# Layer 0's sink column written by ScalarE, the first transfers in another order, and the last product in two pieces

## The chip, the cores and the metric

The kernel runs on one core of a Trainium2 chip. The metric is the device time of one execution in microseconds; the median of three runs of the kernel before is 1686.93 us (1686.22 to 1688.71). The core has a matrix engine (TensorE, PE in the profile, with its weight loads as PEld), VectorE (DVE), ScalarE (ACT), GpSimd (POOL) and SyncE (SP), which here issues every transfer between the memories. Each engine works through its own list of instructions in order and waits where one of them needs what another engine or a transfer has not yet delivered.

## What is computed

Two layers over 512 latent tokens and 256 context tokens of width 1024, all in float32. Each layer modulates its input with vectors that come from a conditioning vector (`silu(c) @ w_ada + b_ada`), mixes tokens, normalises, and applies an MLP of width 4096 with a squared ReLU. Layer 0 mixes with windowed attention of 16 query heads over 2 key heads, whose softmax has one more logit per head, the sink, which gives weight to no value:

```python
hx = x * (1.0 + sc1) + sh1
hc = ctx * (1.0 + csc1) + csh1
...
def softmax_with_sink(s, sink):
    m = jnp.maximum(jnp.max(s, axis=-1, keepdims=True), sink)
    p = jnp.exp(s - m)
    return p / (jnp.sum(p, axis=-1, keepdims=True) + jnp.exp(sink - m))
...
x = layer_norm(alpha * x + g1 * ax, ln1_g[i], ln1_b[i])
fx = sqrelu_mlp(x * (1.0 + sc2) + sh2, mlp_w1[i], mlp_w2[i])
x = layer_norm(alpha * x + g2 * fx, ln2_g[i], ln2_b[i])
```

Layer 1 mixes with differential attention. The output is the 512 latent tokens after layer 1.

## The kernel before, in words

**Products.** Every large matrix product is made of three products of reduced precision (`mm3`, lines 321 to 324): a float32 operand is split into a high part (a cast by ScalarE) and a low part (raw minus high, a subtraction by VectorE), and high·high, low·high and high·low are added up in the same accumulator. `wsplit` (line 299) does this for a weight: a transfer into `w_raw`, the cast `w_h`, the subtraction `w_l` (line 312). The helpers `dv`, `ac`, `gp` (lines 259 to 269) issue one instruction on VectorE, ScalarE or GpSimd, so most instructions carry one of the lines 260, 264 and 268 in the profile; tile names tell them apart.

**What sets the order.** A planner (`Flow`, line 63) runs while the program is built. Jobs are generators with priorities; each says what it waits for, and the planner keeps a rough clock in which each instruction of the other engines has an assumed length (`dve`, `act`, `pool2`, `mm`, lines 209 to 222). The job that may go on by that clock writes its matrix products next. So the order on TensorE is fixed by the planner's assumptions. The orders on VectorE, ScalarE, GpSimd and SyncE are set afterwards by the scheduler of the tile framework. An instruction that is added or removed on ScalarE or VectorE in layer 0's attention therefore moves products on TensorE as well.

**The start (lines 736 to 846).** Work goes in four groups `g` of 256 input columns. `start_load(g)` issues four 512 KB pieces of `w_ada` (for the scale and the shift), two pieces of the transposed input `xT` (384 KB each), and, in the groups 0 and 2, half of the key and value weights (`a_wkv`), and always a quarter of the first half of `a_wq`. `ada_stream` (line 348) makes the modulation rows: TensorE products `ada_ps`, a copy `ada_rows` by ScalarE, a transposition `ada_t` by TensorE, which needs the unit matrix `identr` (cast by VectorE from `ident`), and three small VectorE instructions, which need `badaT`. Then `start_x` (line 785) makes `hx`: ScalarE writes the high part, VectorE computes the modulated value in place and then the low part (GpSimd for the context tokens). `kv_job` multiplies each 128-column slice `k` of `hx` with the key and value weights (eighteen products of 256 columns for each slice), `proj` does the queries. All transfers go through SyncE's one list; a transfer takes one of eight semaphores in turn and waits until the one that used it eight transfers earlier has landed.

**Layer 0's attention (`group`, line 974).** 24 groups (6 blocks of 128 queries by 4 quarters of the heads) of four heads. For each head: scores `s_ps` by TensorE; one VectorE instruction that adds the mask, stores the negated scores in `e` and gives their row minimum `nm`, started from the negated sink `nsink` (line 1009); a VectorE maximum that writes the sink's column `e[:, W_]` (line 1012); the exponential by ScalarE over all columns with `nm` as its bias, which also gives the sum (line 1015); a reciprocal on VectorE; the multiplication by it on GpSimd (line 1018). When all four heads are ready, TensorE transposes them (`pT_ps`), ScalarE and VectorE copy the transposed blocks in turn (`pT`), and TensorE multiplies with the values (`o_ps`). Between these, the planner puts query projections, modulation rows for later, and, in `out_proj` (line 1076), the first half of the output projection (`y_ps`, with `yg`, `y_s` and their statistics on VectorE).

**The end (`tok_product`, line 589, and `done4`, line 1554).** The last product of layer 1's MLP takes for each of four token blocks and each half of the 1024 columns 24 products of 512 columns into one accumulator. VectorE multiplies it with the gate (`g_tmp`), adds it to `acc`, and takes the statistics; for the second half of a block `done4` follows: aggregate, a power on GpSimd, two VectorE passes over `acc` and the transfer out.

Of the kernel before, what the change touches and what calls it, by code (L numbers as in the profile page):

```python
# [19 lines left out]
P = 128  # L20
# [214 lines left out]
def hybrid_block(ctx: ExitStack, tc: tile.TileContext, t: dict, out: bass.AP):  # L235
# [23 lines left out]
    def dv(n, deps, fn, lat=LAT, **kw):  # L259
        fn(**kw)  # L260
        return fl.op("D", dve(n), deps, lat)
# [327 lines left out]
    def tok_product(pool, src, W, seq, acc, gates, done=None, st=None, scale=1.0, extra=None, pre={}, sink=None,  # L589
                    late=(1,)):  # L590
# [4 lines left out]
        for i, (half, tb) in enumerate(seq):  # L595
            if half not in Ws:
                Ws[half] = W(half)
            if (half, tb) in pre:
                pt, give, u0 = pre[(half, tb)]
            else:  # L600
                yield sm_.ok
                pt, u0 = psm("y_ps"), 0
                give = lambda x, i=sm_.take(): sm_.give(i, x)
            left = {u for h, b in seq[i + 1:] if h == half for u in range(pre[(h, b)][2] if (h, b) in pre else 0, 4)}
# [45 lines left out]
    def mlp(l, hx, ready, apool, pool, ntok, acc, gates, done, extra, res, XR=0):  # L650
# [25 lines left out]
        for ch in range(4):  # L676
# [52 lines left out]
            if ch == 2:  # L729
# [3 lines left out]
                                   done if ch == 3 else None, extra=extra, sink=sum_up(ch, gates) if ch < 3 else None)  # L733
# [5 lines left out]
    badaT = load_const("badaT", [P, DEPTH, 6, KT], adap[0])  # L739
# [4 lines left out]
    with tc.tile_pool(name="qpool", bufs=6, side="right") as qpool, \  # L744
# [6 lines left out]
        nc.vector.tensor_copy(out=identr, in_=load_const("ident", [P, P], pool))  # L751
# [17 lines left out]
        def start_load(g):  # L769
            Wa = [ada_load(t["w_ada"][0, m, g, u], next(raws)) for m in (1, 0) for u in range(2)]  # L770
            xs = []
            for k in (2 * g, 2 * g + 1):
                x, gr, rr = next(raws)
                x = x[:, 0:TOK]
                xs.append((k, x, dma(TOK, [gr], out=x, in_=t["xT"][:, k]), rr))
            if g == 0:
                Wkv.append(wsplit(t["a_wkv"][0]))
            if g == 2:
                hl = [pool.tile([P, 1024], F32R, name="w_kv", tag="x4", bufs=3) for _ in range(2)]
                Wkv.append(wsplit(t["a_wkv"][1], hl=hl + [None, None]))  # L780
            Wq[0].append(wsplit(t["a_wq"][0, g]))
            return Wa, xs
# [70 lines left out]
        def setup():  # L853
# [3 lines left out]
            nc.sync.dma_start(out=mask, in_=t["mask"])  # L857

        lnT = load_const("lnT", [P, DEPTH, 4, KT])
# [114 lines left out]
        def group(n, tb, qd):  # L974
# [9 lines left out]
            for j in range(4):  # L984
# [21 lines left out]
                else:  # L1006
# [5 lines left out]
                d = dv(1, [d], nc.vector.tensor_tensor, out=e[:, W_:W_ + 1], in0=nsink[:, hd_:hd_ + 1], in1=nm,  # L1012
                       op=ALU.max)
                sm = small.tile([P, 1], F32, name="sm", tag="sm")
                a = ac(W_ + 200, [d], nc.scalar.activation, out=e[:, 0:W_ + 1], in_=e[:, 0:W_ + 1], func=AF.Exp,
# [638 lines left out]
```

## Time and profile before

The profiled execution of the kernel before took 1690.51 us, of which its span from the first to the last instruction is 1688.7 us. A profile row of the timeline gives the start in us, the length, the engine, the line, the operation, what it writes and reads, and, in brackets, how long the engine had been idle and what ended the wait.

| | |
|---|---|
| median of 3 runs | 1686.93 us |
| profiled execution, its span | 1690.51 us, 1688.7 us |
| mean granted TensorE clock in it | 0.991 |
| TensorE (PE) busy | 1617.0 us, 96% of the span |
| VectorE (DVE) busy | 956.7 us, 57% |
| ScalarE (ACT) busy | 658.2 us, 39% |
| GpSimd (POOL) busy | 344.4 us, 20% |

### The profile page before, as it was taken

How to read it: one execution, taken by the hardware profiler on the slowest of the kernel's cores; microseconds unless marked ns; L12 is line 12 of the kernel's file. 1: busy time of each engine (PE TensorE's matmuls, PEld its weight loads, DVE VectorE, ACT ScalarE, POOL GpSimd, SP SyncE). 2: the span in 40 equal slices, each digit the busy share in tenths (PEclk: the TensorE clock that was granted, in tenths of full speed). 3: DMA queues.
4: the chain of work that ended last, by engine and by line, in shares of the span. 5: the costliest groups of instructions: out<-in, count | busy, mean ns of one | idle time of the engine just before them, and what ended most of it. 6: DMA issues, size and time to landing. Idle time of an engine off the chain costs nothing.

```text
span 1688.7 us, 23443 instructions
## 1 busy us (share of the span) xinstructions
PE 1617.0 (96%) x9129; PEld 1392.0 (82%) x9129; DVE 956.7 (57%) x1811; ACT 658.2 (39%) x1281; POOL 344.4 (20%) x314
## 2 busy tenths in 40 slices
PE   6899999999999999999999999999989899999997
PEld 4787677789889889979978998999877788888886
DVE  3665787567756344344446777677656552332436
ACT  3454565362223113202316555555543533222230
POOL 1243544100001101243220223221101001103422
PEclk9999999999999999999999999999999899999999
DMA  9111451434445334234313122211133323132321
GB/s 365 42 51 37 170 175 35 136 125 130 145 138 162 100 125 150 100 113 139 109 59 110 51 69 67 69 45 38 47 113 111 102 80 120 63 125 75 112 88 50
DMA packets 57239, 174.77 MB, mean 103 GB/s; under 512 B 7144, under 2 KB 13096, under 8 KB 57128
## 3 DMA queue, kind: packets, MB, share of 16 engines
q1 hardware_dynamic: 57128, 173.27, 30.6%
q8 instruction: 72, 1.18, 0.3%
q14 instruction: 39, 0.32, 0.1%
HBM read 165.35 MB, written 7.90 MB: 103 GB/s over the span
## 4 chain that ended last, share of the span: by engine, by line
PE 74%; DVE 10%; issue 5%; ACT 4%; DMA 3%; POOL 3%; SPq 0%; POOLq 0%; DVEq 0%; ACTq 0%
PE y_ps L324 10%; PE y_ps L323 10%; PE y_ps L322 10%; PE h_ps L322 8%; PE h_ps L323 8%; PE h_ps L324 8%; PE o_ps L1031 2%; PE qkv_ps L322 2%; PE qkv_ps L323 2%; PE s_ps L1347 2%; PE qkv_ps L324 2%; DVE w_l L312 2%; PE pT_ps L1049 2%; DVE e L260 1%; PE o_ps L1385 1%
## 5 line engine op out<-in xcount | busy, mean ns | idle before, releaser
L264 ACT CAST w_h<-w_raw 128x1024 fp32r<-128x1024 f32 (+1 forms) x185 | 186.4, 1014 | 413.1 <-PE y_ps L324 208.6
L312 DVE TENSOR_TENSOR w_l<-w_raw,w_h 128x1024 fp32r<-128x1024 f32 (+1 forms) x185 | 220.9, 1205 | 220.6 <-ACT w_h L264 219.7
L323 PE MATMUL y_ps<-w_l,hid 128*128 128x512 f32 x640 | 252.9, 395 | 1.8 <-DVE w_l L312 1.7
L324 PE MATMUL y_ps<-w_h,hid 128*128 128x512 f32 x640 | 252.9, 395 | 0.7 <-DVE hid L260 0.7
L322 PE MATMUL y_ps<-w_h,hid 128*128 128x512 f32 x640 | 253.1, 395 | 0.0
L268 POOL TENSOR_TENSOR relu<-relu 128x768 f32<-128x768 f32 (+1 forms) x48 | 80.4, 1674 | 608.2 <-ACT relu L264 608.2
L324 PE MATMUL h_ps<-hx0m,w_l 128*128 128x384 f32 (+1 forms) x528 | 175.7, 333 | 1.6 <-DVE w_l L312 1.6
L322 PE MATMUL h_ps<-hx0m,w_h 128*128 128x384 f32 (+1 forms) x528 | 175.7, 333 | 0.2 <-ACT w_h L264 0.2
L323 PE MATMUL h_ps<-hx0m,w_h 128*128 128x384 f32 (+1 forms) x528 | 175.3, 332 | 0.0
L323 PEld LDWEIGHTS y_ps<-w_l,hid 128*128 128x128 f32 x640 | 120.4, 188 | 31.1 <-DVE w_l L312 3.3
L324 PEld LDWEIGHTS y_ps<-w_h,hid 128*128 128x128 f32 x640 | 120.4, 188 | 30.1 <-DVE hid L260 2.0
L322 PEld LDWEIGHTS y_ps<-w_h,hid 128*128 128x128 f32 x640 | 120.4, 188 | 28.7 <-ACT hid L264 0.4
L322 PE MATMUL qkv_ps<-w_h,hx 128*128 128x384 f32 (+1 forms) x384 | 127.8, 333 | 0.1
L323 PE MATMUL qkv_ps<-w_l,hx 128*128 128x384 f32 (+1 forms) x384 | 123.2, 321 | 0.3 <-DVE w_l L312 0.2
L324 PE MATMUL qkv_ps<-w_h,hx 128*128 128x384 f32 (+1 forms) x384 | 123.0, 320 | 0.0
L268 POOL TENSOR_TENSOR e<-e,sm 128x512 f32<-128x512 f32 (+2 forms) x96 | 94.1, 995 | 115.4 <-DVE sm L260 76.9
L322 PE MATMUL h_ps<-hx1m,w_h 128*128 128x512 f32 (+1 forms) x288 | 107.7, 374 | 3.6 <-ACT relu L264 3.6
L323 PE MATMUL h_ps<-hx1m,w_h 128*128 128x512 f32 (+1 forms) x288 | 107.3, 372 | 0.0
L324 PE MATMUL h_ps<-hx1m,w_l 128*128 128x512 f32 (+1 forms) x288 | 107.2, 372 | 0.0
L324 PEld LDWEIGHTS h_ps<-hx0m,w_l 128*128 128x128 f32 x528 | 99.1, 188 | 2.9 <-DVE w_l L312 2.9
L322 PEld LDWEIGHTS h_ps<-hx0m,w_h 128*128 128x128 f32 x528 | 99.1, 188 | 0.8 <-ACT w_h L264 0.6
L323 PEld LDWEIGHTS h_ps<-hx0m,w_h 128*128 128x128 f32 x528 | 99.1, 188 | 0.1
(225 smaller groups left out, 3112.6 us busy)
## 6 DMA issues: line engine op xcount, KB each, us to landing
w_raw<-in_w SPq DMA_DIRECT2D x128, 512.0 KB, 3.5
w_raw<-in_w_adaT SPq DMA_DIRECT2D x56, 512.0 KB, 3.5
w_raw<-in_w_ada SPq DMA_DIRECT2D x24, 512.0 KB, 4.0
w_raw<-in_b_w SPq DMA_DIRECT2D x32, 384.0 KB, 3.6
raw<-in_w_ada SPq DMA_DIRECT2D x16, 512.0 KB, 9.6
w_raw<-in_a_wq SPq DMA_DIRECT2D x8, 512.0 KB, 4.7
w_raw<-in_a_wo SPq DMA_DIRECT2D x8, 512.0 KB, 3.4
w_raw<-in_b_wo SPq DMA_DIRECT2D x8, 512.0 KB, 3.5
```

What stands on the lines that cost most here:

```text
L260: fn(**kw)
L264: fn(**kw)
L268: fn(**kw)
L312: last["split"] = nc.vector.tensor_tensor(**kw)
L322: nc.tensor.matmul(out=o, lhsT=lh, rhs=rh, start=start, stop=False)
L323: nc.tensor.matmul(out=o, lhsT=lh, rhs=rl, start=False, stop=False)
L324: last["pe"] = nc.tensor.matmul(out=o, lhsT=ll, rhs=rh, start=False, stop=stop)
L1031: nc.tensor.matmul(out=po[odd * HD:odd * HD + HD, 0:256], lhsT=vv[:, kb, kvh], rhs=pt_[:, odd * 256:odd * 256 + 256], start=(i == 0), stop ...
L1049: nc.tensor.transpose(out=pp[:, c * P:(c + 1) * P], in_=es[j][:, i * P:(i + 1) * P], identity=ident)
L1347: nc.tensor.matmul(out=sp[:, c * 512:c * 512 + 384], lhsT=qTt[:, tt, hl, qb * P:(qb + 1) * P], rhs=kS[:, tt, c * 384:c * 384 + 384], start ...
L1385: nc.tensor.matmul(out=po[:, qp * 256:(qp + 1) * 256], lhsT=vt[:, kb, vl], rhs=pt_[:, pl, a * 256:a * 256 + 256], start=(kp == 0 and pl == ...
```

## The change

Three edits, with what they move.

1. **The sink's column.** `nm` is a minimum that starts from `nsink`, so `nm` is never above `nsink`, and the maximum of the two is `nsink` itself. The VectorE maximum is replaced by a ScalarE copy of `nsink` into the column. The copy waits neither for the scores nor for `nm`; the exponential now waits for the scores' VectorE instruction and for the copy.
2. **The first transfers.** `ident` and `badaT` move behind the first four pieces of `w_ada`; the first half of `a_wkv` moves ahead of the first two pieces of `xT`; `lnT` moves behind `mask`, 34 transfers later.
3. **The last product.** The second half of the last token block is computed as two accumulators of 256 columns, each with its own gate and addition on VectorE; the statistics still take all 512 columns at once.

```diff
     def tok_product(pool, src, W, seq, acc, gates, done=None, st=None, scale=1.0, extra=None, pre={}, sink=None,
-                    late=(1,)):
+                    late=(1,), fine=False):
...
+            if fine and i == len(seq) - 1:
+
+                for c in range(2):
+                    if c:
+                        yield sm_.ok
+                        pt = psm("y_ps")
+                        give = lambda x, i=sm_.take(): sm_.give(i, x)
+                    cs_ = slice(half * 512 + c * 256, half * 512 + c * 256 + 256)
+                    tok = slice(tb * P, (tb + 1) * P)
+                    for u in range(4):
+                        w = Ws[half][u]
+                        yield w.t
+                        for k in (2 * u, 2 * u + 1):
+                            c_ = slice((k % 2) * 512 + c * 256, (k % 2) * 512 + c * 256 + 256)
+                            mm3(pt[:, 0:256], hxs(src, k, 0, tok), hxs(src, k, 1, tok), w.h[:, c_], w.l[:, c_], k == 0,
+                                k == KT - 1)
+                        p = fl.pe(6 * mm(256))
...
+                    tm = pool.tile([P, 256], F32, name="g_tmp", tag="tmp", bufs=2)
+                    m = dv(256, [p], nc.vector.tensor_tensor, out=tm, in0=pt[:, 0:256], in1=gates[0][:, cs_], op=ALU.mult)
+                    give(m)
+                    r = dv(256, [m], nc.vector.tensor_tensor, out=acc[tb][:, cs_], in0=acc[tb][:, cs_], in1=tm, op=ALU.add)
+                st[tb], r = stats(acc[tb], half, r, st.get(tb))
+                done(tb, st[tb], r)
+                continue
...
-    badaT = load_const("badaT", [P, DEPTH, 6, KT], adap[0])
+    badaT = adap[0].tile([P, DEPTH, 6, KT], F32, name="c_badaT")
...
-        nc.vector.tensor_copy(out=identr, in_=load_const("ident", [P, P], pool))
...
         def start_load(g):
             Wa = [ada_load(t["w_ada"][0, m, g, u], next(raws)) for m in (1, 0) for u in range(2)]
+            if g == 0:
+                nc.vector.tensor_copy(out=identr, in_=load_const("ident", [P, P], pool))
+                nc.sync.dma_start(out=badaT, in_=t["badaT"])
+                Wkv.append(wsplit(t["a_wkv"][0]))
             xs = []
             for k in (2 * g, 2 * g + 1):
                 x, gr, rr = next(raws)
                 x = x[:, 0:TOK]
                 xs.append((k, x, dma(TOK, [gr], out=x, in_=t["xT"][:, k]), rr))
-            if g == 0:
-                Wkv.append(wsplit(t["a_wkv"][0]))
...
             nc.sync.dma_start(out=mask, in_=t["mask"])
+            nc.sync.dma_start(out=lnT, in_=t["lnT"])
 
-        lnT = load_const("lnT", [P, DEPTH, 4, KT])
+        lnT = const.tile([P, DEPTH, 4, KT], F32, name="c_lnT")
...
-                d = dv(1, [d], nc.vector.tensor_tensor, out=e[:, W_:W_ + 1], in0=nsink[:, hd_:hd_ + 1], in1=nm,
-                       op=ALU.max)
+
+                d = [d, ac(1, [], nc.scalar.copy, out=e[:, W_:W_ + 1], in_=nsink[:, hd_:hd_ + 1])]
                 sm = small.tile([P, 1], F32, name="sm", tag="sm")
-                a = ac(W_ + 200, [d], nc.scalar.activation, out=e[:, 0:W_ + 1], in_=e[:, 0:W_ + 1], func=AF.Exp,
+                a = ac(W_ + 200, d, nc.scalar.activation, out=e[:, 0:W_ + 1], in_=e[:, 0:W_ + 1], func=AF.Exp,
                        scale=-1.0, bias=nm, accum_out=sm)
```

Where the instructions stand changes at three places that the prediction uses. The first is SyncE's list at the very start; `raw` are the buffers for `w_ada` and `xT`. Before:

```order
L283 DMA c_cT<-in_cT 128x16
L283 DMA c_badaT<-in_badaT 128x96
L283 DMA c_ident<-in_ident 128x128
L283 DMA c_lnT<-in_lnT 128x64
L275 DMA raw_119<-in_w_ada 128x1024
L275 DMA raw_121<-in_w_ada 128x1024
L275 DMA raw_123<-in_w_ada 128x1024
L275 DMA raw_125<-in_w_ada 128x1024
L275 DMA raw_127<-in_xT 128x768
L275 DMA raw_129<-in_xT 128x768
L275 DMA w_raw<-in_a_wkv 128x1024
```

And of the change, the same engine from the same place:

```order
L283 DMA c_cT<-in_cT 128x16
L275 DMA raw_114<-in_w_ada 128x1024
L275 DMA raw_116<-in_w_ada 128x1024
L275 DMA raw_118<-in_w_ada 128x1024
L275 DMA raw_120<-in_w_ada 128x1024
L283 DMA c_ident<-in_ident 128x128
L799 DMA c_badaT<-in_badaT 128x96
L275 DMA w_raw<-in_a_wkv 128x1024
L275 DMA raw_132<-in_xT 128x768
L275 DMA raw_134<-in_xT 128x768
```

Three small transfers stood ahead of the first `w_ada`; now none of them does, two follow the fourth `w_ada`, and `a_wkv` has passed both pieces of `xT`. The rest of SyncE's list up to the query weights keeps its order.

The second place is VectorE's list right after the first group's modulation, where it makes the low part of `hx` (`hx_91` before, `hx_90` in the change, from `raw_127` and `raw_129`, now `raw_132` and `raw_134`) and of the weights (`w_l`). Before:

```order
L260 TENSOR_SCALAR raw_127<-raw_127,mods_81 128x512
L260 TENSOR_SCALAR raw_127<-raw_127,mods_81 128x256
L260 TENSOR_TENSOR hx_91<-raw_127,hx_91 128x512
L260 TENSOR_SCALAR raw_129<-raw_129,mods_81 128x512
L260 TENSOR_SCALAR raw_129<-raw_129,mods_81 128x256
L260 TENSOR_TENSOR hx_91<-raw_129,hx_91 128x512
L312 TENSOR_TENSOR w_l<-w_raw,w_h 128x1024 x2
```

And of the change:

```order
L312 TENSOR_TENSOR w_l<-w_raw,w_h 128x1024
L260 TENSOR_SCALAR raw_132<-raw_132,mods_81 128x512
L260 TENSOR_SCALAR raw_132<-raw_132,mods_81 128x256
L260 TENSOR_TENSOR hx_90<-raw_132,hx_90 128x512
L260 TENSOR_SCALAR raw_134<-raw_134,mods_81 128x512
L260 TENSOR_SCALAR raw_134<-raw_134,mods_81 128x256
L260 TENSOR_TENSOR hx_90<-raw_134,hx_90 128x512
L312 TENSOR_TENSOR w_l<-w_raw,w_h 128x1024
```

The first `w_l` (of `a_wkv`) has gone from behind both slices of `hx` to ahead of them. On ScalarE its cast `w_h` has gone the same way, from behind the four instructions for `hx` to ahead of them.

The third place is TensorE's list at the end of layer 0's attention: the transpositions of the last group's heads, and what stands ahead of them. `e_3551`, `e_3585`, `e_3574` and `e_3625` are the last group's four heads before. Before:

```order
L1049 MATMUL pT_ps<-identr,e_3540 128x128
L998 MATMUL s_ps<-kT_117,qT_1791 128x256 x2
L1031 MATMUL o_ps<-pT,v_118 64x256 x4
L1049 MATMUL pT_ps<-identr,e_3551 128x128
L1049 MATMUL pT_ps<-identr,e_3585 128x128
L1049 MATMUL pT_ps<-identr,e_3574 128x128
L1049 MATMUL pT_ps<-identr,e_3625 128x128
```

And of the change, where the last group's heads are `e_3551`, `e_3593`, `e_3562` and `e_3604`; right ahead of the first row stand the scores of the last two heads (`s_ps`, four products) and then the six `y_ps` products of 512 columns of which this is the last:

```order
L324 MATMUL y_ps<-w_h,hx_93 128x512
L1078 MATMUL pT_ps<-identr,e_3473 128x128
L1078 MATMUL pT_ps<-identr,e_3516 128x128
L1078 MATMUL pT_ps<-identr,e_3484 128x128
L1078 MATMUL pT_ps<-identr,e_3527 128x128
L1060 MATMUL o_ps<-pT,v_113 64x256 x4
L1078 MATMUL pT_ps<-identr,e_3551 128x128
L1078 MATMUL pT_ps<-identr,e_3593 128x128
L1078 MATMUL pT_ps<-identr,e_3562 128x128
L1078 MATMUL pT_ps<-identr,e_3604 128x128
```

Between the last scores and the last group's transpositions stood four `o_ps` products; now six `y_ps` products, four transpositions of the group before and four `o_ps` products stand there. On VectorE, the scores of the last head stood behind `yg`, `y_s`, a `pT` copy and the statistics of an output block, with the low part of an `hx` between them and the maximum; in the change the scores of the last two heads follow each other directly. Between the start and this place many products of the two lists trade places; behind it the two lists of TensorE are the same up to the last product.

More of the change, by code (lines that the diff above doesn't have):

```diff
@@ L732, in mlp @@
                                    [(h_, tb) for h_ in range(2) for tb in range(ntb)], acc, gates,
[L733 removed]
+                                   done if ch == 3 else None, extra=extra, sink=sum_up(ch, gates) if ch < 3 else None,
+                                   fine=l == 1 and ch == 3)
     l0 = ExitStack()
```

2 lines of the change are left out of this document (added).

## The prediction

> **What bounds the kernel now.** First the page's engine totals.
>
> ```profile
> PE 1617.0 (96%) x9129; PEld 1392.0 (82%) x9129; DVE 956.7 (57%) x1811; ACT 658.2 (39%) x1281; POOL 344.4 (20%) x314
> ```
>
> TensorE is busy 96% of the span. No product is removed, so the change can win only the time in which TensorE waits (1688.7 − 1617.0 = 71.7 us), and only at the three places that it touches: the start, layer 0's attention, the tail. Next the timeline of the first 31 us:
>
> ```profile
> 1.19 0.42 SPq L283 DMA_DIRECT2D c_badaT<-in_badaT  x1
> ...
> 2.60 1.85 SPq L275 DMA_DIRECT2D raw<-in_w_ada  x4
> 3.58 0.23 DVE L751 CAST identr<-c_ident 128x128 fp32r<-128x128 f32 x1 [2.42 <-DMA c_ident<-in_ident]
> ...
> 8.17 1.08 PE L364 MATMUL ada_ps<-raw,cs 128*32 128x256 f32 x8 [0.56 <-DMA raw<-in_w_ada]
> 9.75 0.69 PE L388 MATMUL ada_t<-identr,ada_rows 128*128 128x128 f32 x2 [0.49 <-ACT ada_rows L264]
> 12.37 0.37 ACT L264 COPY ada_rows<-ada_ps 128x256 f32<-128x256 f32 x1 [2.67 <-PE ada_ps L364]
> ...
> 13.92 2.50 ACT L264 ACTIVATE hx<-raw,mods 128x512 fp32r<-128x512 f32 x4 [1.18 <-DVE mods L260]
> 14.77 0.91 DVE L260 TENSOR_SCALAR raw<-raw,mods 128x512 f32<-128x512 f32 x2 [0.88 <-ACT hx L264]
> 15.59 0.68 DVE L260 TENSOR_TENSOR hx<-raw,hx 128x512 fp32r<-128x512 f32 x1
> 16.33 1.98 ACT L264 CAST w_h<-w_raw 128x1024 fp32r<-128x1024 f32 x2
> 17.99 2.88 DVE L312 TENSOR_TENSOR w_l<-w_raw,w_h 128x1024 fp32r<-128x1024 f32 x2
> 19.79 0.58 PE L323 MATMUL kv_ps<-w_l,hx 128*128 128x256 f32 x1 [1.79 <-DVE w_l L312]
> 20.16 0.41 PE L324 MATMUL kv_ps<-w_h,hx 128*128 128x256 f32 x1
> 30.27 1.22 DVE L312 TENSOR_TENSOR w_l<-w_raw,w_h 128x1024 fp32r<-128x1024 f32 x1
> ```
>
> The first key and value products wait for the weight's low part, which VectorE makes only after both slices of `hx`. The third product, the first that needs a low `hx`, starts at 20.16; from there the timeline shows no such wait of TensorE until the stage ends near 58. Then its waits from 60 to 320 us, and ScalarE's longest from 60 to 313:
>
> ```profile
> PE pT_ps L1049 <- ACT pT L264: 2.9, 4, 0.9
> PE pT_ps L1049 <- POOL e L268: 2.2, 1, 2.2
> PE s_ps L994 <- DVE nm L260: 1.8, 3, 0.9
> ```
>
> ```profile
> ACT e L264 <- DVE e L260: 53.5, 45, 2.3
> ```
>
> The softmax is slow as a chain (ScalarE waits 53.5 us for VectorE, the maximum being the last link), but the planner puts other products under it, so only 6.9 us reach TensorE. The largest wait is the last group's:
>
> ```profile
> 309.40 0.47 DVE L260 CUSTOM_DVE_ANT_0 e<-s_ps,mask,nsink 128x256 f32<-128x256 f32 x1
> 309.52 0.55 PE L1049 MATMUL pT_ps<-identr,e 128*128 128x128 f32 x3
> ...
> 310.05 0.42 DVE L260 TENSOR_TENSOR hx<-o_ps,hx 128x256 fp32r<-128x256 f32 x1 [0.17 <-ACT hx L264]
> 310.39 0.15 DVE L260 TENSOR_TENSOR e<-nsink,nm 128x1 f32<-128x1 f32 x1
> 310.63 0.51 ACT L264 ACTIVATE e<-e,nm 128x257 f32<-128x257 f32 x1 [0.62 <-DVE e L260]
> ...
> 311.57 0.61 POOL L268 TENSOR_TENSOR e<-e,sm 128x256 f32<-128x256 f32 x1 [2.25 <-DVE sm L260]
> 312.24 0.77 PE L1049 MATMUL pT_ps<-identr,e 128*128 128x128 f32 x5 [2.17 <-POOL e L268]
> ```
>
> Three transpositions run, the fourth waits 2.17 us for its head. Four slices show what such a wait can cost beside itself (PE busy is the first number after the length, the granted clock PEclk the third from the end):
>
> ```profile
> 309.97:313.37 3.40, 0.99 (x8) 0.66 (x9) 0.98 (x4) 1.23 (x4) 0.61 (x1) 1.00 0.25 76
> 313.40:316.80 3.40, 3.40 (x12) 1.93 (x11) 0.76 (x2) 0.38 (x1) 0.00 (x0) 0.50 0.00 0
> 364.58:367.98 3.40, 1.72 (x15) 1.75 (x16) 2.76 (x6) 3.12 (x11) 0.00 (x0) 1.00 0.32 118
> 368.00:371.40 3.40, 3.40 (x32) 3.40 (x31) 1.39 (x4) 3.40 (x11) 0.00 (x0) 1.00 0.00 0
> ```
>
> After 3.4 us with TensorE busy for 0.99, the clock is halved for 3.4 us: 1.7 us lost. After 3.4 us with 1.72 busy it isn't.
>
> **The start.** Once the first modulation rows are done (13.92), VectorE now makes `w_l` first. Alone it takes 1.22 (row 30.27): 15.14. ScalarE's cast, half of 1.98, fits between the end of `ada_rows` (12.74) and 13.92. Then the two modulations (0.82 to the next start, 15.59 − 14.77) and the low `hx` (0.68): 15.14 + 0.82 + 0.68 = 16.64 for the third product, against 20.16: 3.5 us earlier. The second slice's low part follows some 1.8 us later on VectorE, while eighteen products run.
>
> The transfers must keep this up. One row of the slices gives their rate (last number, GB/s):
>
> ```profile
> 19.80:23.20 3.40, 3.40 (x16) 3.40 (x17) 1.07 (x1) 0.00 (x0) 0.00 (x0) 1.00 1.03 407
> ```
>
> 512 KB at 407 GB/s take 1.29 us. The first `w_ada` is issued at 1.19 in place of 2.60, 1.41 earlier. The second landed at 8.17; now 6.76, the fourth two lengths later at 9.34, `ident` (64 KB, 0.16) at 9.50, its cast (0.23) at 9.73: just about when the transpositions start now (9.75). They stay where they are, and what the head start gives TensorE's first products is lost again to `ident`. `a_wkv` lands about 1.3 later, near 11, in time for the cast. The next groups' pieces, 1.4 earlier, meet a TensorE that is 3.5 earlier; the first of the second group lands after two `xT`, one `a_wq` and itself, near 15.5, while its use stands behind eighteen products that start at 16.64, so this holds. I take 3.3 of the 3.5 for an `ident` that is a little late. Bounds: 1.4 (only the head start) and 3.6. `lnT` and `badaT` cost nothing: `badaT` lands with `ident`, `lnT` is needed only in the MLP.
>
> **The sink's column.** What goes, and what bounds the copy, which the trace does not show:
>
> ```profile
> L260 DVE TENSOR_TENSOR e<-nsink,nm 128x1 f32<-128x1 f32 x96 | 22.4, 247 | 0.5
> ```
>
> ```profile
> 3.84 0.19 ACT L1197 CAST id<-identr 4x4 fp32r<-4x4 f32 x1 [1.27 <-DVE identr L751]
> ```
>
> ```profile
> 60.26 0.27 ACT L264 COPY v<-kv_ps 128x128 f32<-128x128 f32 x1 [3.46 <-PE kv_ps L324]
> ```
>
> VectorE loses 22.4 us, all beside products. ScalarE gains 96 copies of 0.19 (nearest in size) to 0.27: 18 to 26 us, below the 53.5 that it sits waiting for VectorE; their cover is that idle time, and without it all would queue in front of the exponentials. [...]
>
> For the last group: now 309.40 to 312.24 is 2.84 us, of which the low `hx` and the maximum take 310.63 − 309.95 = 0.7. In the change the last two heads' scores follow each other on VectorE, 0.47 more for the second: about 2.6 from its start. Ahead of the transpositions TensorE has six 512-column products, four transpositions and four `o_ps` of 256 columns. At 0.23 and 0.12 (rows under the tail) and 0.11 for a transposition (0.77 for five less 0.55 for three, halved) that is 1.4 + 0.4 + 0.5 = 2.3, in place of the 0.5 of four `o_ps`. So 0.3 of the 2.17 is left: a gain of 1.9. The halved clock then mostly goes: 1.7 in this execution, but the stretches may lie differently in another run. If the trigger lies at about 1.7 idle of 3.4 (1.68 idle did not do it above), a 2.17 wait reaches it in about two cuts of three, so 1.1 against the median.
>
> [...]
>
> For all other groups I take zero: the waits on `pT` and `nm` (2.9 + 1.8) shrink with an earlier exponential, and new ones come from the copies and the re-planned order. Bounds: −4.7, and +4 (as much again the other way).
>
> **The tail.**
>
> ```profile
> 1679.61 0.39 PE L323 MATMUL y_ps<-w_l,hid 128*128 128x512 f32 x1
> 1679.84 0.40 PE L324 MATMUL y_ps<-w_h,hid 128*128 128x512 f32 x1
> 1680.28 0.69 DVE L563 TENSOR_TENSOR g_tmp<-y_ps,g2x 128x512 f32<-128x512 f32 x1
> ...
> 1681.73 0.69 DVE L260 BATCH_NORM_STATS2 bn<-acc 128x6 f32<-128x512 f32 x1
> ```
>
> After the last product (products 0.23 apart) two VectorE steps of 0.72 stand ahead of the statistics. With 256 columns they take some 0.45 (0.42 for 256 columns, row 310.05): 0.54 saved. The same columns in 48 products in place of 24 may cost a little more; between these two rows lie three products of 256 columns:
>
> ```profile
> 48.35 0.29 PE L322 MATMUL kv_ps<-w_kv,hx 128*128 128x256 f32 x1
> 48.71 0.28 PE L322 MATMUL kv_ps<-w_kv,hx 128*128 128x256 f32 x1
> ```
>
> 48 × 0.12 = 5.8 against 24 × 0.23 = 5.5: up to 0.3, of which I take 0.2. Net 0.3 (bounds 0 to 0.5); the first half's steps stand beside the second half's products.
>
> **The sum.** 3.3 + 1.9 + 1.1 + 0 + 0.3 = 6.6 us. The profiled execution (1690.51) would come to 1690.51 − 6.6 − 0.6 for its own full clock loss = 1683.3; it lies 3.6 above the median of the runs, so the median goes from 1686.93 to 1680.3. What is late next is VectorE's part in the start and the weights' low parts of the output projection, both unchanged.
>
> **The rivals.**
>
> *The attention gives nothing (chance 0.23).* New waits in the re-planned order eat the end's gain. For: 6.9 us of waits were all that reached TensorE, and the planner's guess of 0.07 for a copy is under 0.19. Against: the longer cover ahead of the last transpositions stands in the list. 1686.93 − 3.3 − 0.3 = 1683.3.
>
> *ScalarE blocks (0.05), slower.* A copy waits until its `e` buffer is free, in order, and behind it stand `pT` copies on which TensorE waits; today's four such waits cost 0.7 each. If every group had one more, 24 × 0.7 = 16.8, less the 6.6 won: +10, 1697. [...] It decides from 15 such groups on (15 × 0.7 = 10.5: 3.9 slower net). Against: ScalarE is idle 53.5 us there.
>
> *The start is bound by its transfers (0.14).* `ident` or the next pieces come later than worked out, and only 1.4 is won: 1682.2.
>
> *The change doesn't do what it says (0.02).* Another order hides everything: 1686.9.
>
> **How the numbers follow.** My forecast, 1680.3, has the remaining 0.56. The range: all bounds for the good side give 1686.93 − 3.6 − 1.9 − 1.7 − 2.5 (half of the 4.7) − 0.5 = 1676.7; for the other side, the attention 0.5 worse than now and half of the start (1.7) give 1686.93 − 1.7 + 0.5 = 1685.7; beyond it lie the blocking, the last rival and some of the third. About 0.2% (3.4 us, so 1683.6) is what a measurement can tell from no change. Faster: most of the forecast (0.52), of the transfers' rival (0.11) and half of the first (0.12): 0.75. Slower: 0.05. Same: 0.20.
>
> **What would show it.** Third key and value product near 16.6, first transpositions near 9.8; the wait for the last group's head under 0.7 and no half clock behind it; the waits on `pT` and `nm` together no longer than 4.7; `g_tmp` to statistics 0.9. If the third product stands later than 18.5, the start failed; if TensorE's waits from 60 to 313 exceed today's by over 5, ScalarE blocks.

## The result

Five runs of the changed kernel have a median of 1674.51 us (1671.59 to 1679.03), five of the kernel before on the same chip 1687.63 (1686.22 to 1688.96). The ratio is 0.9919, 95% interval [0.9905, 0.9933]: 13.1 us faster. The direction was forecast, the size was not: the gain is about twice the 6.6 us, and the median lies below the range (1676.7 to 1685.7).

The profiled execution took 1671.59 us, the shortest of its five, while that of before (1690.51) lay above its median. The two profiles therefore differ by 18.9 us, and the sum of their stages is not the effect of the change. First the engine totals of the page after:

```profile
PE 1609.0 (96%) x9153; PEld 1387.8 (83%) x9153; DVE 935.4 (56%) x1717; ACT 669.1 (40%) x1377; POOL 344.2 (21%) x314
```

TensorE waits for 1669.8 − 1609.0 = 60.8 us, 10.9 less than before; and it is busy for 8.0 less, with 24 products more. Waits alone are not the whole story: the clock has a part in it (mean granted clock 0.991 before, 0.995 here). The start, from the timeline of after:

```profile
1.19 1.84 SPq L275 DMA_DIRECT2D raw<-in_w_ada  x4
...
9.58 0.66 PE L388 MATMUL ada_t<-identr,ada_rows 128*128 128x128 f32 x2 [2.14 <-DVE identr L798]
13.61 1.22 DVE L312 TENSOR_TENSOR w_l<-w_raw,w_h 128x1024 fp32r<-128x1024 f32 x1
16.27 0.58 PE L324 MATMUL kv_ps<-w_h,hx 128*128 128x256 f32 x1 [0.80 <-DVE hx L260]
...
21.59 0.37 PE L324 MATMUL kv_ps<-w_h,hx 128*128 128x256 f32 x1
21.80 0.28 PE L322 MATMUL kv_ps<-w_h,hx 128*128 128x256 f32 x1
21.92 0.28 PE L323 MATMUL kv_ps<-w_l,hx 128*128 128x256 f32 x1
```

The third key and value product stands at 16.27 (forecast 16.64, before 20.16), the first transpositions at 9.58, and they wait 2.14 us for `identr`, as forecast. The last rows show something that the forecast left out: products stand 0.21 apart up to 21.80 and 0.12 from there. TensorE gets its full clock only there, 5.5 us after the third product (the record of the granted clock begins with 1.00 at 21.78); before, it got it at 23.24, 3.1 us after. In this pair the lead of 3.9 us at the third product is down to 2.1 at the stage's last product, where 3.3 was forecast.

The last group of layer 0's attention, same view:

```profile
299.16 0.40 PE L322 MATMUL y_ps<-w_h,hx 128*128 128x512 f32 x1
299.37 0.19 ACT L264 COPY e<-nsink 128x1 f32<-128x1 f32 x1
299.74 0.51 ACT L264 ACTIVATE e<-e,nm 128x257 f32<-128x257 f32 x1 [0.17 <-DVE nm L260]
...
301.66 0.61 POOL L268 TENSOR_TENSOR e<-e,sm 128x256 f32<-128x256 f32 x1 [0.36 <-DVE sm L260]
302.16 0.65 PE L1060 MATMUL o_ps<-pT,v 128*64 128x256 f32 x4 [0.42 <-DVE pT L260]
302.74 1.09 PE L1078 MATMUL pT_ps<-identr,e 128*128 128x128 f32 x8
```

The eight transpositions follow the `o_ps` products without a wait; the 2.17 us are gone, and no half clock follows (granted clock 1.00 from 300 to 306.8). In their place the second half of the `o_ps` products waits 0.42 us for a copied `pT`, of which more below. The waits from 60 to 330 us, first TensorE's, then ScalarE's longest for `e`:

```profile
PE s_ps L1023 <- DVE nm L260: 2.3, 4, 0.9
PE ada_t L388 <- ACT ada_rows L264: 1.5, 1, 1.5
PE q_ps L322 <- DVE rope L260: 1.5, 1, 1.5
PE ada_ps L364 <- DMA w_raw<-in_w_ada: 1.2, 1, 1.2
PE pT_ps L1078 <- ACT pT L264: 0.6, 1, 0.6
...
ACT e L264 <- DVE nm L260: 25.4, 27, 2.1
```

`pT` and `nm` together are down to 2.9 (0.6 + 2.3). ScalarE waits 25.4 us for `nm`, where it waited 53.5 for the maximum. All waits of TensorE in this window fall from 13.8 to 8.4 us. The tail:

```profile
1661.66 0.28 PE L324 MATMUL y_ps<-w_h,hid 128*128 128x256 f32 x1
...
1662.04 0.42 DVE L260 TENSOR_TENSOR g_tmp<-y_ps,g2x 128x256 f32<-128x256 f32 x1
1662.48 0.42 DVE L260 TENSOR_TENSOR acc<-acc,g_tmp 128x256 f32<-128x256 f32 x1
1662.94 0.69 DVE L260 BATCH_NORM_STATS2 bn<-acc 128x6 f32<-128x512 f32 x1
```

`g_tmp` to statistics is 0.90, as forecast.

### The profile page after: what moved, and what is told of

Its sections match the earlier page's. It is cut to its first block, busy times and chain, and to the rows that moved or that the text cites. A ratio compares the mean times of both kernels' runs of the same rounds, so it can differ in the third digit from the quotient of the medians.

```text
span 1669.8 us, 23525 instructions
## 1 busy us (share of the span) xinstructions
PE 1609.0 (96%) x9153; PEld 1387.8 (83%) x9153; DVE 935.4 (56%) x1717; ACT 669.1 (40%) x1377; POOL 344.2 (21%) x314
## 4 chain that ended last, share of the span: by engine, by line
PE 76%; DVE 9%; issue 5%; ACT 4%; DMA 3%; POOL 3%; SPq 0%; DVEq 0%; POOLq 0%; ACTq 0%
PE y_ps L324 10%; PE y_ps L323 10%; PE y_ps L322 10%; PE h_ps L322 8%; PE h_ps L323 8%; PE h_ps L324 8%; PE qkv_ps L322 2%; PE qkv_ps L323 2%; PE qkv_ps L324 2%; PE o_ps L1060 2%; PE s_ps L1376 2%; PE pT_ps L1078 2%; DVE w_l L312 2%; PE o_ps L1414 1%; PE s_ps L1027 1%
## 5 line engine op out<-in xcount | busy, mean ns | idle before, releaser
L323 PE MATMUL y_ps<-w_l,hid 128*128 128x512 f32 (+1 forms) x648 | 254.2, 392 | 1.8 <-DVE w_l L312 1.7
L324 PE MATMUL y_ps<-w_h,hid 128*128 128x512 f32 (+1 forms) x648 | 254.2, 392 | 0.4 <-DVE hid L260 0.2
L322 PE MATMUL y_ps<-w_h,hid 128*128 128x512 f32 (+1 forms) x648 | 254.3, 392 | 0.0
```

What stands on the lines that cost most here:

```text
L322: nc.tensor.matmul(out=o, lhsT=lh, rhs=rh, start=start, stop=False)
L323: nc.tensor.matmul(out=o, lhsT=lh, rhs=rl, start=False, stop=False)
L324: last["pe"] = nc.tensor.matmul(out=o, lhsT=ll, rhs=rh, start=False, stop=stop)
```

## The experiments

Theory A: the sink's edit won far more than forecast, since the waits of all groups shrank, because the chain to the exponential is a link shorter (A1). Rivals: the new order of the products does it (A2), the transfers do it (B), the half-clock stretches merely fell otherwise (C). Each kernel was timed beside the kernel before, whose medians in the four sets were 1689.02, 1688.70, 1689.49 and 1689.01. "Attention" is the time in its one profile from the last key and value product to the first transposition of a normalised row, read from the timeline; "of it half clock" is half the length of the half-clock stretches in it (in the one of before, products of 512 columns stand 0.42 us apart, and 0.23 right behind it), "waits" all TensorE waits from 60 to 330 us.

| kernel | median us | ratio to before [95%] | attention | of it half clock | waits |
|---|---|---|---|---|---|
| before | | | 279.1 | 1.7 | 13.8 |
| changed (`after_again`) | 1675.83 | 0.9921 [0.9905, 0.9938] | 269.7 | 0 | 7.7 |
| `sink_alone` | 1680.76 | 0.9961 [0.9949, 0.9974] | 270.0 | 0 | 7.9 |
| `transfers_alone` | 1684.54 | 0.9978 [0.9966, 0.9990] | 279.5 | 3.4 | 13.3 |
| `last_alone` | 1687.54 | 0.9987 [0.9976, 0.9999] | 277.6 | 0 | 13.7 |
| `no_last` | 1675.88 | 0.9920 [0.9905, 0.9936] | 269.7 | 0 | 7.7 |
| `copy_old_order` | 1682.97 | 0.9968 [0.9957, 0.9980] | 275.3 | 3.4 | 9.3 |
| `max_new_order` | 1689.32 | 1.0006 [0.9994, 1.0018] | 278.9 | 0 | 14.3 |
| `two_copies` | 1677.79 | 0.9932 [0.9915, 0.9949] | 270.7 | 0 | 8.5 |
| `ident_first` | 1675.97 | 0.9920 [0.9904, 0.9937] | 270.1 | 0 | 8.1 |
| `before_filled` | 1686.81 | 0.9987 [0.9975, 0.9998] | 276.8 | 0 | 11.7 |
| `warm_end` | 1677.16 | 0.9926 [0.9913, 0.9938] | 271.3 | 0 | 9.3 |
| `max_beside` | 1666.91 | 0.9872 [0.9855, 0.9888] | 271.1 | 0 | 9.7 |
| `moved_128` | 1668.30 | 0.9884 [0.9863, 0.9905] | 268.7 | 0 | 7.8 |
| `before_moved_128` | 1678.92 | 0.9943 [0.9924, 0.9962] | 278.5 | 3.4 | 13.0 |
| `moved_64` | 1669.41 | 0.9884 [0.9864, 0.9905] | 270.0 | 0 | 8.5 |
| `moved_256` | 1678.17 | 0.9939 [0.9919, 0.9958] | 270.3 | 0 | 8.0 |

**The parts alone.** The first three kernels have one edit of the change each; `no_last` is the changed kernel with `fine=False`.

> The sink edit alone, on the kernel before; TensorE's order is the changed one through the attention. Theory A (the attention won far more than the 1.9 us forecast, because the waits of all groups shrank): 6 to 9 us faster than the kernel before, the last attention product (o_ps) about 7 earlier, TensorE's waits between 60 and 330 us down from 13.8 to 9 or less. Rival B (the first transfers gave most of it): 2 to 4 us faster. Rival C (the half-clock stretches merely fell otherwise): the waits shrink by 2 at most, and the rest of the difference stands in the mean granted clock.

> The first transfers alone, in the changed order; the sink's maximum and the last product as before. Theory A: 2 us faster (the key and value stage ends 2.1 earlier, as in the changed kernel's profile, since the full clock came only at 21.8), attention waits unchanged at about 13.8. Rival B (the start gives most): 4 us faster or more. Rival E (what the start wins is lost again later to waits for transfers): within 1 us.

> The last product in two pieces alone. Theory A: 0.3 to 0.7 us faster, from the last product to the end 0.7 less; within what the measurement can tell. Rival: the 24 additional products cost what the shorter end gives, no difference.

> The changed kernel with the last product in one piece, as before. If the 2.2 us that the split showed alone are its own, this is 2 us slower than the changed kernel; if the trace is right, which shows 0.7 from the last product to the end, it is 0.3 to 0.8 slower, which can't be told from none.

By the ratios, of 1689 us: the sink 6.6 us (4.4 to 8.6), the transfers 3.7 (1.7 to 5.7), the last product 2.2 (0.2 to 4.1). B is out. The sink and the transfers add up to 10.3 us (7.4 to 13.2 if their errors are independent), while both together, `no_last`, win 13.5 (10.8 to 16.0): within what can be told the parts add up. In the trace of `sink_alone` the last `o_ps` comes 7.4 earlier than before, the waits are 5.9 less: theory A's numbers. The last product's 2.2 are not borne out: without it, `no_last` takes as long as the changed kernel, and in the traces the time from the start of the last product to the end falls by 0.6 (8.71 in `no_last`, 8.12 in `after_again`). The 24 additional products cost 0.2 of that: from the first of these products to the end it is 14.08 and 13.69, 0.4 less.

**The link or the order.** In `copy_old_order` the planner is told the old instruction, in `max_new_order` the new one, so each takes one half of the sink's edit:

```diff
-                d = dv(1, [d], nc.vector.tensor_tensor, out=e[:, W_:W_ + 1], in0=nsink[:, hd_:hd_ + 1], in1=nm,
-                       op=ALU.max)
+                nc.scalar.copy(out=e[:, W_:W_ + 1], in_=nsink[:, hd_:hd_ + 1])
+                d = fl.op("D", dve(1), [d])
```

> ScalarE's copy in place of VectorE's maximum, but the planner is told the old instruction, so TensorE's order is that of the kernel before, product by product. Theory A1 (the shorter chain to the exponential gives it): 4 to 7 us faster, the wait for the last group's head falls from 2.17 to about 1.5. Rival A2 (the re-planned order gives it): under 2 us faster, the 2.17 stays above 1.4. Rival D (ScalarE blocks once nothing is moved around it): slower by 1 or more.

```diff
-                d = dv(1, [d], nc.vector.tensor_tensor, out=e[:, W_:W_ + 1], in0=nsink[:, hd_:hd_ + 1], in1=nm,
-                       op=ALU.max)
+                nc.vector.tensor_tensor(out=e[:, W_:W_ + 1], in0=nsink[:, hd_:hd_ + 1], in1=nm, op=ALU.max)
+                d = [d, fl.op("A", act(1), [])]
```

> VectorE's maximum stays, but the planner is told ScalarE's copy, so TensorE's order is that of the sink edit, product by product. Theory A1 (shorter chain): within 2 us of the kernel before, since the order was planned for a shorter chain and new waits on the heads come up. Rival A2 (re-planned order): 5 to 8 us faster, nearly as much as the sink edit alone; no wait over 1 us on the last group's heads.

A1 holds: 5.4 us faster (3.4 to 7.3) with the old order, nothing with the new order alone. Taken without the half clock, the attention is 277.4 before, 271.9 with the copy in the old order, 270.0 with both: 5.5 us for the shorter chain, 1.9 more for the order that relies on it. TensorE's waits in `copy_old_order`:

```profile
PE s_ps L994 <- DVE nm L260: 1.9, 2, 1.2
...
PE pT_ps L1049 <- POOL e L268: 1.5, 1, 1.5
PE y_ps L323 <- DVE w_l L312: 1.3, 1, 1.3
PE pT_ps L1049 <- ACT pT L264: 0.7, 2, 0.5
```

The wait for the last group's head is 1.5 where it was 2.17: the link's own 0.6. The waits for `pT` fell from 2.9 to 0.7 without any other order. With the new order and the old chain most of them stay (2.2), and those on `nm` double:

```profile
PE s_ps L994 <- DVE nm L260: 3.7, 5, 1.4
PE pT_ps L1049 <- ACT pT L264: 2.2, 3, 1.0
...
PE pT_ps L1049 <- POOL e L268: 1.4, 3, 0.6
...
PE o_ps L1031 <- DVE pT L260: 1.1, 1, 1.1
```

**The copies' price.** `two_copies` issues each sink copy of the changed kernel twice:

```diff
                 d = [d, ac(1, [], nc.scalar.copy, out=e[:, W_:W_ + 1], in_=nsink[:, hd_:hd_ + 1])]
+                nc.scalar.copy(out=e[:, W_:W_ + 1], in_=nsink[:, hd_:hd_ + 1])
```

> The changed kernel with each of the 96 sink copies issued twice on ScalarE (the planner is told one; TensorE's order is the same). Theory A (the copies lie in ScalarE's idle time): 0 to 1.5 us slower than the changed kernel. Rival D (the copies sit in the way on ScalarE and the change wins in spite of them): 3 us slower or more, with TensorE's waits on pT up by as much, and a version without any copy would then win that much again.

The copies have one row among the groups of instructions of after (96 in all, mean in ns; the idle time before them and what ended it stand behind the bar):

```profile
L264 ACT COPY e<-nsink 128x1 f32<-128x1 f32 x96 | 15.5, 189 | 5.3 <-DVE nsink L260 2.6 <-PE pT_ps L1078 2.4
```

0.189 us, the lower end of the forecast's bounds. 96 more of them cost 1.0 us of attention in the trace and 2.0 in the medians, whose intervals overlap. That lies between the two expectations (up to 1.5, or 3 and more), but TensorE's wait for `pT` stays as it was (0.7 and 0.6): the rival of the blocked ScalarE is out. `max_beside` lets VectorE compute the maxima of the changed kernel again, into a cell of its own:

```diff
+                mx = small.tile([P, 1], F32, name="mx", tag="mx")
+                nc.vector.tensor_tensor(out=mx, in0=nsink[:, hd_:hd_ + 1], in1=nm, op=ALU.max)
```

> The changed kernel, in which VectorE also makes the 96 maxima as before, but into a cell that nobody reads: VectorE's 22 us of small work come back, the chain to the exponential stays short. TensorE's order is that of the changed kernel. Theory A1 (the link taken out of the chain is what counts): within 1.5 us of the changed kernel. Rival F (the time freed on VectorE is what counts): 4 to 6 us slower than the changed kernel, and TensorE's waits from 60 to 330 us up by 3 or more.

This came out as nobody had expected: 9 us faster than the changed kernel. It could not be read before the cause was found (the place of the tiles, below). Against `moved_128`, which has the same place and no maxima, it takes as long (1666.91 and 1668.30). In the traces its attention is 2.4 us longer and its waits 1.8, but one wait makes up this 1.8, in `max_beside` and in `moved_128`:

```profile
PE ada_t L388 <- ACT ada_rows L264: 2.3, 1, 2.3
```

```profile
PE ada_t L388 <- ACT ada_rows L264: 0.5, 1, 0.5
```

This wait lies anywhere between 0.5 and 2.3 us in the profiles with this order, and is 2.3 in `warm_end` too, which has no maxima. So by these profiles at most some 0.6 of the 7.4 us can be put down to the time freed on VectorE; the chain and its order give the rest.

**The clock.** `before_filled` puts products into the 2.17 us wait of before:

```diff
+                        if n == 23 and i == 0 and c == 3:
+                            for _ in range(14):
+                                nc.tensor.matmul(out=pp[:, 3 * P:4 * P], lhsT=identr, rhs=identr, start=True, stop=True)
```

> The kernel before, with 14 products of 128 columns that nobody reads put into the 2.17 us wait for the last group's head (into the accumulator that the waiting transposition overwrites). The wait stays. Theory (waiting longer than about 1.7 us halves the clock for 3.4 us, which the prediction put at 1.1 us on average): no half-clock stretch near 313 us in the profile, median 0.5 to 1.5 us faster than the kernel before, not to be told from none. Rival: the stretch has another cause and stays.

Its timeline and its slices (PE busy, and the granted clock third from the end):

```profile
309.51 1.76 PE L1051 MATMUL pT_ps<-identr 128*128 128x128 f32 x14
311.93 0.77 PE L1052 MATMUL pT_ps<-identr,e 128*128 128x128 f32 x5 [0.65 <-POOL e L268]
```

```profile
309.90:313.30 3.40, 2.51 (x22) 1.95 (x21) 1.06 (x4) 1.19 (x3) 0.61 (x1) 1.00 0.19 65
313.30:316.70 3.40, 3.40 (x19) 2.38 (x16) 0.55 (x2) 1.31 (x2) 0.00 (x0) 1.00 0.00 0
```

The head is about as late as before, 0.65 of its wait is left behind the small products, and the clock stays up. The ratio says 2.2 us (0.3 to 4.2), more than the 0.5 to 1.5 expected. In the four profiles that have this wait and nothing in it (before, `transfers_alone`, `last_alone`, `before_moved_128`) the loss there is 1.7, 3.4, 0 and 3.4: 2.1 on average.

> The changed kernel once more, for a second profile and five more times. Theory (the half-clock stretches of layer 1 fall where the clock's windows happen to cut the same waits): the waits of TensorE in layer 1 come out the same within 0.1 us each, while the stretches at half clock lie at other places than in the first profile; median 1673 to 1676, and runs with a mean granted clock 0.001 lower take about 1.7 us more. Rival (the change itself took the stretches of layer 1 away): only the two stretches of the first profile come back, at 1179 and 1292.

Layer 1's waits come out the same (1.71 and 1.71, 2.33 and 2.32, 1.94 and 1.96 us), the stretches do not: 1179 and 1292 in the first profile, 1041, 1181 and 1294 in the second. Of the six runs the two at a mean clock of 0.994 and 0.995 took 1673.6 us, the two at 0.991 1677.2 and 1679.2. The first of these waits, in the first profile:

```profile
1039.61 0.34 PE L1280 MATMUL kT_ps<-identr,sk 128*128 128x128 f32 x2 [1.71 <-DVE sk L260]
```

In the profile of before and in this first one every change of the granted clock lies a whole number of steps of 3.41 us behind the start of its record (before: 85 steps from 23.24 to the first half-clock stretch at 313.4; here: 339 from 21.78 to the one at 1178.9). These steps are the windows meant here. The slices about the wait, cut at them, in the first profile and then in the second:

```profile
1035.60:1039.00 3.40, 2.31 (x21) 2.17 (x19) 2.90 (x5) 2.63 (x7) 1.46 (x2) 1.00 0.00 0
1039.00:1042.40 3.40, 2.32 (x16) 2.08 (x16) 1.81 (x7) 1.45 (x4) 1.48 (x2) 1.00 0.11 39
```

```profile
1037.59:1041.00 3.41, 1.70 (x15) 1.59 (x14) 2.68 (x4) 1.68 (x5) 1.75 (x3) 1.00 0.11 38
1041.00:1044.42 3.42, 2.82 (x13) 2.32 (x12) 1.58 (x5) 1.44 (x3) 1.00 (x2) 0.50 0.24 73
```

The same wait falls into two windows in one execution (2.31 and 2.32 of 3.4 busy, nothing happens) and into one in the other (1.70 busy, halved). So half an idle window sufficed here (1.70 busy of 3.41), as 2.41 idle of 3.40 did in the prediction's row. Nor do these rows show a sharp limit by busy time: 1.72 busy of 3.42 halved the clock in `copy_old_order`, 1.72 of 3.40 did not in the prediction's other row; and in the first profile 2.31 of 3.41 (1175.49 to 1178.90) halved it, where 2.31 and 2.32 above did not. C is true of the two profiles of before and after, where layer 1's stretches differ by some 5 us, but not of most of the 13.1 (the sum below). `ident_first` shows that the change doesn't take them away: it has the changed kernel's order, and its profile has stretches at 1041, 1178 and 1239 too.

```diff
         nc.vector.tensor_copy(out=cs[:, :, 0:2], in_=sig)
+        nc.vector.tensor_copy(out=identr, in_=load_const("ident", [P, P], pool))
...
             if g == 0:
-                nc.vector.tensor_copy(out=identr, in_=load_const("ident", [P, P], pool))
                 nc.sync.dma_start(out=badaT, in_=t["badaT"])
```

> The changed kernel with ident ahead of the first w_ada instead of behind the fourth; TensorE's order is the same. Theory (the late ident holds the first transpositions 2.14 us): the transpositions start about 1.5 earlier, near 8.1, and the third key and value product near 15, so the stage ends up to 1.3 earlier: 0.5 to 1.3 us faster than the changed kernel. Rival (the full clock comes at a fixed time after TensorE's first steady work, and the rows' own transfers bound the start): within 0.5.

Its transpositions and third product:

```profile
8.60 0.69 PE L388 MATMUL ada_t<-identr,ada_rows 128*128 128x128 f32 x2 [0.49 <-ACT ada_rows L264]
...
15.40 0.58 PE L324 MATMUL kv_ps<-w_h,hx 128*128 128x256 f32 x1 [0.80 <-DVE hx L260]
```

Both are 0.9 to 1.0 earlier; the 0.5 to 1.3 us expected of it did not show: the time is that of the changed kernel within what can be told.

`warm_end` fills the four waits behind layer 1's output projection in `ln_job` with 5, 11, 16 and 5 small products into an accumulator of their own:

```diff
+            if warm.get((tb, q)):
+                wp = psS("warm")
+                for _ in range(warm[(tb, q)]):
+                    nc.tensor.matmul(out=wp[:, 0:P], lhsT=identr, rhs=identr, start=True, stop=True)
```

> The changed kernel with 37 products of 128 columns that nobody reads, in the four waits (0.91, 1.48, 2.10, 0.76 us) for the normalised rows behind layer 1's output projection. All profiles so far show 10.24 us at half clock there, which is 5.1 us. Theory (the stretch comes from these waits alone): no half clock there, 3 to 5 us faster than the changed kernel, near 1671. Rival (the small products do not count as load, or they delay the rows): the stretch stays, and the time is that of the changed kernel or up to 2 us more.

The slice from the first transposition to the first product of the MLP, changed kernel and `warm_end`:

```profile
1286.78:1297.53 10.75, 5.51 (x34) 4.29 (x32) 10.26 (x21) 8.55 (x25) 1.20 (x2) 0.72 0.28 98
```

```profile
1296.59:1307.01 10.42, 8.16 (x71) 7.65 (x69) 9.93 (x21) 8.17 (x24) 1.19 (x2) 1.00 0.32 101
```

The half clock is gone, as the theory said; won are 0.33 us here. My 5.1 us were wrong: TensorE is busy for half of this slice only, and VectorE (10.26 of 10.75) sets its length. The last 4.2 us of the stretch lay in the MLP's first products, which come faster (at half clock those of 256 columns stand 0.21 us apart in the changed kernel, 0.12 from 301.88 on; from its first product to its last 364.1 us in the changed kernel, 362.3 in `warm_end`). That makes 2.2 us in these two traces; the medians show no gain (1677.16 against 1675.83).

**The place of the tiles.** An unused tile of the pool `small`, of 4, 2 or 8 cells of 32 bytes, written once:

```diff
+                if n == 0 and j == 0:
+                    nc.vector.memset(small.tile([P, 1], F32, name="mx", tag="mx", bufs=4), 0.0)
```

> The changed kernel with one unused tile of four cells, which takes 128 bytes in every partition and so moves all tiles behind it (hx, hid, oT, acc and the rest; not the weight buffers w_raw, w_h, w_l) by 128 bytes, as the cell of max_beside did. One VectorE instruction more, TensorE's order as in the changed kernel. Theory G (the place of the tiles made max_beside faster, not its maxima): products of 512 columns whose moving operand is a weight stand 227 to 228 ns apart instead of 232, and the time is 1664 to 1668; max_beside's maxima then cost 0 to 1.5 us. Rival (the maxima themselves changed something): as the changed kernel, 1674 to 1677.

> The kernel before with the same unused tile. Theory G: 7 to 10 us faster than the kernel before, near 1679, and the distance between the two moved kernels is again 11 to 15 us, so that the change's gain has nothing to do with where its tiles lie. Rival: the kernel before does not get faster by it, and the place is one more thing that the change touches.

> The changed kernel with the unused tile of 64 bytes instead of 128. If any move between the weights and the operands that VectorE and ScalarE write helps, 227 ns and 1664 to 1668; if it is 128 bytes that count, 232 ns and 1674 to 1677. I know no reason for the one or the other.

> The changed kernel with an unused tile of 256 bytes. If the pace goes with the distance in a pattern of 128 bytes that repeats every 256, this is back at 232 ns and 1674 to 1677; if more distance is better, 227 ns or less and 1668 or less.

The MLPs' products of 512 columns, from the groups of before, `moved_128` and `moved_256` (count, busy us, mean ns of one):

```profile
L322 PE MATMUL y_ps<-w_h,hid 128*128 128x512 f32 x640 | 253.1, 395 | 0.0
```

```profile
L322 PE MATMUL y_ps<-w_h,hid 128*128 128x512 f32 x632 | 246.6, 390 | 0.0
```

```profile
L322 PE MATMUL y_ps<-w_h,hid 128*128 128x512 f32 x632 | 250.0, 396 | 0.2 <-ACT hid L264 0.2
```

A product is 5 ns shorter in `moved_128`, and there are some 1900 of this form: 9 us. By the ratios the move wins 6.2 us in the changed kernel (0.9921 and 0.9884) and 9.6 in the kernel before (0.9943). Theory G holds: 128 bytes help both kernels, 64 help too, 256 give nothing. In the two kernels themselves `hid`, `oT`, layer 0's `hx` and the weight buffers are built at the same addresses, and a product takes 395 ns in both, so none of the 13.1 us comes from this. (In layer 0's attention the changed kernel has `kT`, `v` and the mask 512 bytes lower. `transfers_alone` has them so too, and the old attention, 276.1 us without the half clock.) With both moved, the medians stand 10.6 us apart (ratios 0.9884 and 0.9943), a little less than the 11 to 15 expected, and within their intervals of the 13.1. The fastest version without the useless maxima is `moved_128`, 1668.30 us.

## Why the prediction was too small

**The start (3.3): the steps were right, the gain at the stage's end is 0.7 smaller.** Each step stands in the trace within 0.4 us. The stage's end is 2.6 earlier on average (61.0 in seven profiles with the old transfers, 58.5 in nine with the new; `ident_first` and `warm_end` left out), while the third product is 3.6 earlier. The full clock came at 24.2 and 21.3 on average, so it follows the third product by 4.2 before and by 4.8 in the change; that eats some 0.3 us. The rest of the loss was not looked into. The timed 3.7 (1.7 to 5.7) holds both numbers.

**The last group (1.9) and the clock behind it (1.1).** All of the 2.17 us are gone, where 0.3 was to be left. The cover was worked out from the right rows of the list, but is longer: from the six products to the last transpositions TensorE takes 3.6 us (299.16 to 302.74) and not 2.3, since the `o_ps` products take 1.2 (0.65 and 0.58) and not 0.5, and 0.42 go into the wait for `pT`. The clock's term was too small: 2.1 us by the profiles and 2.2 by `before_filled`. The guess that two cuts in three halve the clock held (three of four), but two of them lost two windows, not one.

**"For all other groups I take zero": this step failed.** Without the half clock the attention is 7.4 us shorter with the sink's edit (277.4 to 270.0); the last group's wait is 2.2 of that, and some 5 come from the groups where the forecast had none. The forecast let the shrinking waits be balanced by new ones. But the waits on `pT` fell from 2.9 to 0.6, and to 0.7 by the shorter chain alone, while the new ones (`s_ps` on `nm`, 1.8 to 2.3) came, but small. The bound of 4.7 counted only the waits on `pT` and `nm`. Others of the same window in before, and then what is left in `sink_alone`:

```profile
PE y_ps L323 <- DVE w_l L312: 1.5, 2, 1.3
PE ada_t L388 <- ACT ada_rows L264: 1.4, 2, 0.8
PE o_ps L1031 <- DVE pT L260: 0.9, 2, 0.6
```

```profile
PE ada_t L388 <- ACT ada_rows L264: 0.9, 1, 0.9
PE pT_ps L1049 <- ACT pT L264: 0.6, 1, 0.6
PE o_ps L1031 <- DVE pT L260: 0.4, 1, 0.4
```

The wait of `o_ps` for the copied `pT` fell with the shorter chain (0.3 in `copy_old_order`, 1.1 in `max_new_order`). That for `w_l` went with the new order: it is gone in `max_new_order` too and stays in `copy_old_order` (1.3). That for `ada_rows` says nothing, as it lies between 0.5 and 2.3 in the profiles with the new order. And waits, with the clock, were taken for all that could be won: attention less waits fell by 1.6 us beside the clock (279.1 − 13.8 − 1.7 = 263.6 to 270.0 − 7.9 = 262.0 in `sink_alone`), so products also stood closer together. Why they did was not looked into.

**ScalarE blocks (0.05)** didn't happen: a copy costs 0.189 us and stands in idle time (96 more of them cost 1.0 us of attention). **The transfers' rival** didn't happen either: the start's steps came up to 0.4 us earlier than worked out, and it gave 2.6, not 1.4.

**The tail (0.3): right**; 0.6 shorter less 0.2 for the products is 0.4.

**The sum.** 2.6 for the start, 8.7 for the attention with its clock (278.7 on average in the three profiles with the open wait and the old place, 270.0 in four with the sink's edit and the old place: both profiles of the changed kernel, `sink_alone`, `no_last`), 0.4 for the tail: 11.7 of 13.1. The rest lies behind layer 0's attention or in the scatter. The changed kernel's 11 runs have a mean granted clock of 0.9931, the 76 of before beside the experiments 0.9906. That is 0.0025 of 1680, 4.2 us, of which 2.1 belong to the removed wait. Whether the other 2 are chance or a lasting difference in how layer 1's waits fall into the windows was not settled: in one and the same order the time from the first normalised row to the end went from 1340.7 (`after`) to 1347.8 us (`ident_first`).

## What to carry to other kernels

A link that is taken out of a dependent chain can shorten waits in every group, and it lets the planner choose another order that shortens more of them. So bound the gain by all waits on those engines in the stage, not only by the rows that name the chain, and set a term to zero only with a reason. The halved clock is priced by what TensorE would have done in the stretch: about 2 us for the lone wait ahead of dense products, 0.33 us in the 10.75 in which it waited for VectorE anyway. Of two profiles, subtract the half-clock stretches before stages are compared.

## What was not expected of the hardware

The pace of 512-column products went with where the operands lie: `y_ps` from `hid` takes 395 ns a product with the kernel's placement (before and after), 390 with `hid` 128 bytes further on and all but one of the weight buffers in place (`moved_128`), 391 to 393 with 64 (`moved_64`), and 395 to 396 with 256 bytes (`moved_256`), while no instruction that writes or reads them changed. `h_ps` from `hx1m`, whose place did not change, takes 395 ns with and without the 128 bytes. Why was not looked into. And TensorE reached its lasting full clock between 19.4 and 25.6 us over these profiles (23.24 before, 21.78 after), 2.6 to 6.2 us after the third key and value product (3.1 before, 5.5 after); the end of the first stage lay between 60.4 and 61.5 us in the seven with the old transfers.
